# Operand sums, gate quarters and sample attention moved to other places in a written-out order

## The chip, the cores and the metric

The kernel runs on one core of a Trainium2 chip. The metric is the device time of one execution in microseconds. TensorE (PE, with PEld for its weight loads) multiplies, VectorE (DVE) and ScalarE (ACT) do the elementwise work, and SyncE (SP) issues every DMA. "L97" in the profile is the line of a helper that records nearly all operations, so the rows are told apart by the names of their tiles.

## The reference

One layer of a hybrid decoder for 1024 prompt positions and 8 samples of 8 new tokens, 1088 rows in all. With `x` of width 2048:

```python
proj = jnp.einsum('bld,de->ble', x, w_in)
gb, gc, h, z_c, q, k, v, z_a, gate_c, gate_a = jnp.split(proj, SPLIT_OFFSETS, axis=-1)
conv_out, conv_state = short_conv(gc * h, conv_prev, conv_w)
y_c = jax.nn.silu(z_c) * gb * conv_out
o, k_state, v_state = attend_fn(q, k, v)
y_a = jax.nn.silu(z_a) * o
merged = (jax.nn.sigmoid(gate_c) * jnp.einsum('blc,cd->bld', y_c, w_conv_out)
          + jax.nn.sigmoid(gate_a) * jnp.einsum('bla,ad->bld', y_a, w_attn_out))
out = jnp.einsum('bld,de->ble', merged, w_out)
y = layer_norm(ALPHA * x + out, ln_g, ln_b)
```

Attention has 16 heads of 64 on 4 key heads, a window of 128, sinks and ALiBi. Samples also read cached keys and values, and the updated caches are outputs.

## The kernel before

**Units.** The projections are made by 100 units that run one after the other. Each is a 2 x 2 block product done with seven products in place of eight (sums of blocks on both sides). In units a0 to a41 half of the input channels are multiplied, for 42 pairs of column blocks; in b0 to b41 the other half is added; m0_0 to m0_7 and m1_0 to m1_7 multiply the convolution's and the attention's result by their output weights. A product is 24 matmuls of 128 x 272 in four *groups* of six, so a unit has 28 groups. Every number is split into a high and a low part, and a product takes three matmuls for a block. The tiles follow the names: `psa37a`, `psa37b` and `psa37c` are the three accumulators of unit a37, `wra`, `wrb` and `wrm` raw weights, `wa`, `wb` and `wm` split weights, `wsa` and so on their sums, `ca`, `cb` and `cm` the unit's result, `xab`, `xdb`, `xcb` and `xbb` the four operand blocks of stage b and `xam` to `xbm` those of stage m.

**Order.** The class `InOrder` wraps PE, DVE, ACT and SP's queue (`te`, `ve`, `se`, `dq`): each engine issues in the order in which the program is written. `tick()` stands behind each group, counts it in `clock`, runs what the agenda has for this number (`after(n, f)`: n groups from now), and takes one piece from `line`, a list of small DVE and ACT steps. So an instruction that waits for a DMA on DVE holds up all that is written behind it for DVE. In `run`, weights are split three products ahead of their use; a product's accumulator is taken out (`take`) after the first group of the next product, and products 2, 4 and 6 add to the accumulator that has just been taken out, so they wait for it. A unit's raw weights are loaded in the third group of the unit before.

**Operands.** `ahead_of(ops)` loads the four blocks of an operand, 16 loads of 272 KB, and puts the eight sums of `combine` on `line`. It is called by the `begin` of a37 (for stage b), of b23 (`gate_unit(13, open_merge)`, for m0) and of m0_4 (for m1). The operand is split into its seven forms (`put`) during the last unit before its stage: a41, b25 and m0_7.

**Merge.** In m0 and m1 each quarter of a unit's result that is finished (by products 1, 4, 5 and 6) is multiplied on DVE by a quarter of the sigmoid gates (`sg`), and in m1 the quarter of m0's result (`cmo`) is added. `gated` issues these loads from its `taken`, which is called when a product is taken out. The last products' results go to `mgd`, from which the output projection (tiles `yr`, `m`, `ms`, weights `wraw` and `wo`, sums `o`) reads.

**Attention and samples.** Prompt attention runs between the units' groups, in 64 steps 15 groups apart. Step s loads its query and key tiles (`qt`, `kt`) at its start, multiplies scores (`sc`) 14 groups later, loads values (`vt`) at 22 and uses them (`po`) at 34. Beside the first eight gate units, b10 to b17, eight sample steps run; each is begun by `after(16, ...)` from its unit's `begin`. The first opens the pool of samples too: it transposes the new keys and values and issues `store`, ten groups after, which writes the caches with 20 DMAs, two of them whole-cache copies in DRAM (`out_k_s<-in_ck`, `out_v_s<-in_cv`).

Of the kernel before, what the change touches and what calls it, by code (L numbers as in the profile page):

```python
# [9 lines left out]
F32 = mybir.dt.float32  # L10
# [7 lines left out]
P = 128  # L18
# [6 lines left out]
HALF = T // 2  # L25
# [25 lines left out]
def tile_hybrid_step(  # L51
# [8 lines left out]
    def pool(name, bufs=1, space=None, stack=None, side=None):  # L60
        kw = {} if space is None else {"space": space}
        if side is not None:
            kw["side"] = side
        if space is not DRAM:
            kw["reuse_waits"] = "tile"
        return (stack or ctx).enter_context(tc.tile_pool(name=name, bufs=bufs, **kw))
# [54 lines left out]
    def at(step, what):  # L121
        assert step > clock[0]
        agenda.setdefault(step, []).append(what)

    def after(groups, what):
        at(clock[0] + groups, what)
# [33 lines left out]
    def slot(shape, dt, name):  # L160
        i = turn_of[0] % (NX if ring[1] is None else SLOTS)
        turn_of[0] += 1
        full = ring[i >= NX].tile([P, T], dt, name=name, tag=f"slot{i}")
        return full[:, : shape[0] * shape[1]].rearrange("p (a b) -> p a b", a=shape[0])

    class Operands:
# [29 lines left out]
        def combine(self, k):  # L196

            line.append(lambda: ve.tensor_sub(self.t3[k], self.t2[k], self.t3[k]))
            line.append(lambda: ve.tensor_add(self.t2[k], self.t3[k], self.b11[k]))
# [227 lines left out]
    def ahead_of(ops):  # L427

        ops.load_all()
        for k in range(4):  # L430
            ops.combine(k)

    todo = []
    for p in range(2, len(PAIRS)):
# [10 lines left out]
    pools = {}  # L445
# [124 lines left out]
    class Step:  # L570
# [116 lines left out]
        def gated(self):  # L687
            ve.tensor_mul(self.o, self.o, self.sz)
            dq.dma_start(yd[8 + self.j][:, TS + self.blk * P : TS + (self.blk + 1) * P], self.o)
# [9 lines left out]
    def gate(d, c):  # L699
        def sigmoid(f):  # L700
            se.activation(c[:, f], c[:, f], AF.Sigmoid)

        after(1, lambda: sigmoid(0))
        after(4, lambda: sigmoid(1))
        after(6, lambda: dq.dma_start(sgd[d], c))
# [4 lines left out]
    def open_samples():  # L710
        sp = pools["sample"] = pool("sample", stack=sam)
        kn = late["kn"] = sp.tile([TS, 2, P], F32, name="kn")
        vn = late["vn"] = sp.tile([TS, 2, P], F32, name="vn")

        tn = late["tn"] = sp.tile([32, 160], F32, name="tn")
        ve.memset(tn, 0.0)
        kl = sp.tile([P, 2, P], F32, name="kl")
        klast, vlast, qkvs, ident = (late[n] for n in ("klast", "vlast", "qkvs", "ident"))

        def turned(i):  # L720
            t = aux(f"pko{i}")
            te.transpose(t[:, 0:P], klast[:, i, :], ident)
            te.transpose(t[0:TS, P : 2 * P], qkvs[:, 8 + i, :], ident)
            te.transpose(t[0:TS, 2 * P : 3 * P], qkvs[:, 10 + i, :], ident)

            def copies():
                se.copy(kl[:, i, :], t[:, 0:P])
                se.copy(kn[:, i, :], t[0:TS, P : 2 * P])
                se.copy(vn[:, i, :], t[0:TS, 2 * P : 3 * P])

            after(2, copies)

        def store():
            dq.dma_start(k_p, kl.rearrange("p a b -> p (a b)"))
            dq.dma_start(v_p, vlast.rearrange("p a b -> p (a b)"))
            for src, old, dst in ((kn, ck, k_s), (vn, cv, v_s)):
                for b in range(NS):
                    dq.dma_start(
                        dst[b, WIN - ST :, :],
                        src[b * ST : (b + 1) * ST].rearrange("p a b -> p (a b)"),  # L740
                    )
                dq.dma_start(dst[:, : WIN - ST, :], old[:, ST:, :])

        after(2, lambda: turned(0))
        after(6, lambda: turned(1))
        after(10, store)
# [200 lines left out]
    def project(p, end, begin=None):  # L947
        u = Unit(f"b{p}", win[p, 1], x1, add=pd[p], begin=begin, end=end)
        todo.append(u)
        return u  # L950
# [19 lines left out]
    def gate_unit(d, begin=None):  # L970
        return project(GT + d, lambda c: gate(d, c), begin)

    def samples(i):
        if i == 0:
            heads_st.close()
            open_samples()
        sample(i // 2, i % 2)

    for i in range(8):
        gate_unit(i, lambda i=i: after(16, lambda: samples(i)))  # L980
    gate_unit(8)

    def open_conv():
# [15 lines left out]
            gate_unit(9 + ct // 2)  # L999


    mst = ExitStack()
    xm = [None, None]

    def open_merge():
        con.close()
        keep.close()
        pools["merge"] = pool("merge", side="right")
        stage = pool("mstage", stack=mst, side="right")
        for b in range(2):  # L1010
            xm[b].stage = stage
        ahead_of(xm[0])
# [4 lines left out]
    gate_unit(14)  # L1017
    x1.leaves = (gate_unit(15), xm[0])

    def gated(b, i):  # L1020

        pos = {1: (0, 0), 4: (1, 1), 5: (1, 0), 6: (0, 1)}
        tiles = {}

        def fetch(q):
            f, h = pos[q]
            hs = slice(h * HALF, (h + 1) * HALF)
            t = tiles[q] = [pools["merge"].tile([P, HALF], F32, name=f"sg{b}_{i}_{q}", tag="sg", bufs=2)]
            dq.dma_start(t[0], sgd[i + 8 * f][:, b, hs])
            if b:  # L1030
                t.append(pools["merge"].tile([P, HALF], F32, name=f"cmo{i}_{q}", tag="cmo", bufs=2))
                dq.dma_start(t[1], cmd[i][:, f, hs])

        def taken(u, n):
            if n == 0:
                fetch(1)
            if n == 2:
                fetch(4)
            if n == 3:
                fetch(5)  # L1040
            if n == 4:
                fetch(6)
            if n not in pos:
                return
            f, h = pos[n]
            v = u.c[:, f, h * HALF : (h + 1) * HALF]
            t = tiles.pop(n)
            after(1, lambda: ve.tensor_mul(v, v, t[0]))
            if b:
                after(2, lambda: ve.tensor_add(v, v, t[1]))  # L1050
            if n == 6:
                after(3, lambda: dq.dma_start((mgd if b else cmd)[i], u.c))

        return taken

    def open_out():
        mst.close()
        pools["oraw"] = pool("oraw", side="right")

    for b, w in enumerate((wc, wa)):  # L1060
        for i in range(8):
            u = Unit(f"m{b}_{i}", w[i], xm[b], taken=gated(b, i))
            if (b, i) == (0, 4):
                u.begin = lambda: ahead_of(xm[1])
            if (b, i) == (0, 7):
                xm[0].leaves = (u, xm[1])
            if (b, i) == (1, 1):
                u.begin = open_out
            todo.append(u)
# [5 lines left out]
    ps, mq = PS["ps"], pools["oraw"]  # L1075

    def split(hi, lo, raw):
        nc.scalar.copy(hi, raw)  # L1078
        nc.vector.tensor_sub(lo, raw, hi.bitcast(F32))  # L1079
# [4 lines left out]
    ORDER = [k for i in range(8) for k in (i, i + 8)]  # L1084

    def weight(k, n):
        raw = mq.tile([P, 512], F32, name="wraw", tag="wraw", bufs=3)
        nc.sync.dma_start(raw, wo[k * P : (k + 1) * P, n * 512 : (n + 1) * 512])
        w = wpool.tile([P, 2, 512], F32R, name="wo", tag="w", bufs=5)
        split(w[:, 0], w[:, 1], raw)  # L1090
        return w[:, 0], w[:, 1]

    units.close()
    op = pool("out")
    ring[1] = op
# [4 lines left out]
    def operand(gi, k):  # L1100
        t0, tn = GROUPS[gi]
        raw = mq.tile([P, tn], F32, name=f"yr{gi}_{k}", tag="yr", bufs=3)
        nc.sync.dma_start(raw, mgd[k % 8][:, k // 8, t0 : t0 + tn])
        m = slot([2, 512], F32R, f"m{gi}_{k}")
        skip = tn - 512
        split(m[:, 0], m[:, 1], raw[:, skip:])
        if skip:
            split(ms[:, k, 0:TS], ms[:, k, TS:], raw[:, 0:TS])
        return m
# [96 lines left out]
    m = {k: operand(0, k) for k in ORDER}  # L1206
# [20 lines left out]
    for i, o in enumerate(outs):  # L1227
        t = clock[0] + 1 + 3 * i
# [16 lines left out]
        for o, a in zip(outs, acc):  # L1245
            o.residual(n, a)
    for k in ORDER:
        raw = mq.tile([P, 512], F32, name="wraw", tag="wraw", bufs=3)
        nc.sync.dma_start(raw, wo[k * P : (k + 1) * P, 3 * 512 :])
        if len(last) < 12:  # L1250
            w = slot([2, 512], F32R, f"l{k}")
        else:
            w = wpool.tile([P, 2, 512], F32R, name=f"l{k}", tag="w", bufs=5)
        split(w[:, 0], w[:, 1], raw)
        last[k] = w
    for i, o in enumerate(outs):
        halves = (slice(0, 256), slice(256, 512)) if i == 3 else (slice(0, 512),)
        for h, c in enumerate(halves):
            acc = banks(f"o1_3_{i}_{h}", 1)[0]
            for kk, k in enumerate(ORDER):  # L1260
                w = last[k]
# [81 lines left out]
```

## Time and profile before

| | |
|---|---|
| three runs | 2747.66 us median, 2744.4 to 2748.97 |
| profiled execution | 2749.23 us, span 2747.1 us |
| mean granted clock of TensorE | 0.988 |
| PE busy | 2646.6 us, 96% |
| DVE busy | 1756.7 us, 64% |
| ACT busy | 1058.9 us, 39% |
| DMA | 415.97 MB, mean 151 GB/s |

In a list of waits, a row says which engine with which tile waited for whom, then the total in us, the times, and the longest. In a timeline, a row has the start, the length, the engine, line and operation, the tiles, and in brackets the idle time of the engine before it and what ended it. In a table of stretches, the columns are the busy time and number of instructions of PE, PEld, DVE, ACT and POOL, and then the granted clock, the busy share of the DMA engines and GB/s.

### The profile page before, as it was taken

Reading aid. Unit: us, or ns where it says so; the run is one execution under the profiler, and the core shown is the slowest. Engines: PE = TensorE matmul, PEld = TensorE weight load, DVE = VectorE, ACT = ScalarE, POOL = GpSimd, SP = SyncE. Lnnn points to the kernel's source line nnn. Section 1 sums busy time; section 2 is a strip of 40 time slices with the busy share of each in tenths; the row PEclk is TensorE's granted clock in tenths of the full one; section 3 lists DMA queues with packets and bytes.
Section 4 is the critical chain, followed back from the end, with each engine's and each line's share of the span. In section 5 each row is a group of like instructions: output and inputs, shape, how many; then the busy total and the mean of one; then the engine's idle time right before and its main releaser. Section 6 shows DMA issues by size and latency. Waiting matters only on the chain.

```text
span 2747.1 us, 47820 instructions
## 1 busy us (share of the span) xinstructions
PE 2646.6 (96%) x19426; PEld 2548.5 (93%) x19426; DVE 1756.7 (64%) x3371; ACT 1058.9 (39%) x2074; POOL 0.2 (0%) x4
## 2 busy tenths in 40 slices
PE   8999999999989999989999999998999999899997
PEld 7999999999989999989989999998999999688886
DVE  7444444444444878878878898887765877533836
ACT  5222322232223446555654555543432423322221
POOL 0000000000000000000000000000000000000000
PEclk9999999999999999999999999999999999999999
DMA  4322332232242366665554545445345566733543
GB/s 161 110 96 96 114 109 96 96 118 105 96 160 96 142 214 207 203 196 164 185 165 141 176 145 163 160 154 202 139 144 209 195 212 199 254 98 113 182 141 103
DMA packets 167328, 415.97 MB, mean 151 GB/s; under 512 B 23443, under 2 KB 75667, under 8 KB 139173
## 3 DMA queue, kind: packets, MB, share of 16 engines
q1 hardware_dynamic: 167108, 412.92, 45.1%
q8 instruction: 153, 2.51, 0.4%
q14 instruction: 67, 0.54, 0.1%
HBM read 295.33 MB, written 119.48 MB: 151 GB/s over the span
## 4 chain that ended last, share of the span: by engine, by line
PE 73%; DVE 14%; ACT 6%; DMA 5%; issue 2%; SPq 1%; DVEq 0%; ACTq 0%
PE o L97 11%; DVE cb L97 2%; DVE wb L97 1%; DMA yr<-mgd 1%; ACT wb L97 1%; ACT p L97 1%; DMA wraw<-in_wo 1%; PE psm_5a L97 1%; PE psm_1a L97 1%; PE psm_6a L97 1%; PE psm_2a L97 1%; ACT L97 1%; PE psm_4a L97 1%; DVE nm L97 1%; DVE wsb L97 1%
## 5 line engine op out<-in xcount | busy, mean ns | idle before, releaser
L97 PE MATMUL o<-wo,m 128*128 128x512 f32 x1344 | 320.9, 394 | 0.2 <-DVE r L1156 0.2
L97 PEld LDWEIGHTS o<-wo,m 128*128 128x128 f32 x1344 | 255.0, 190 | 56.0 <-issue 0.6
L97 DVE TENSOR_TENSOR wa<-wra,wa 128x512 fp32r<-128x512 f32 x210 | 144.4, 689 | 213.3 <-ACT wa L97 213.3
L97 ACT CAST wb<-wrb 128x512 fp32r<-128x512 f32 x210 | 127.3, 615 | 158.3 <-DVE wrb L97 153.4
L1079 DVE TENSOR_TENSOR wo<-wraw,wo 128x512 fp32r<-128x512 f32 x112 | 76.7, 687 | 150.8 <-ACT wo L1078 150.8
L97 DVE TENSOR_TENSOR wb<-wrb,wb 128x512 fp32r<-128x512 f32 x210 | 143.6, 684 | 42.8 <-ACT wb L97 41.1
L1078 ACT CAST wo<-wraw 128x512 fp32r<-128x512 f32 x112 | 69.3, 621 | 222.3 <-PE o L97 173.5
L97 ACT CAST wa<-wsa 128x512 fp32r<-128x512 f32 x84 | 52.2, 621 | 259.4 <-DVE wsa L97 259.4
L97 ACT CAST wa<-wra 128x512 fp32r<-128x512 f32 x210 | 126.3, 621 | 49.2 <-DVE wra L97 47.2
L97 DVE TENSOR_TENSOR wa<-wsa,wa 128x512 fp32r<-128x512 f32 x84 | 58.0, 691 | 92.3 <-ACT wa L97 92.2
L97 ACT CAST wb<-wsb 128x512 fp32r<-128x512 f32 x84 | 51.6, 614 | 155.9 <-DVE wsb L97 154.0
L97 ACT ACTIVATE p<-p,nm 128x256 f32<-128x256 f32 (+1 forms) x128 | 62.4, 489 | 83.7 <-DVE nm L97 83.6
L97 DVE TENSOR_TENSOR wb<-wsb,wb 128x512 fp32r<-128x512 f32 x84 | 57.7, 687 | 33.2 <-ACT wb L97 33.0
L97 ACT ACTIVATE p<-p,den 128x256 f32<-128x256 f32 (+1 forms) x128 | 56.5, 489 | 58.1 <-DVE den L97 56.6
L97 ACT ACT_TABLE_LOAD x58 | 74.4, 1283 | 1.7 <-PEq L1321 0.7
L97 ACT CAST wm<-wrm 128x512 fp32r<-128x512 f32 x80 | 48.4, 621 | 60.9 <-DVE wrm L97 60.7
L97 DVE TENSOR_TENSOR wm<-wrm,wm 128x512 fp32r<-128x512 f32 x80 | 55.1, 688 | 25.2 <-ACT wm L97 24.4
L97 DVE TENSOR_TENSOR cm<-cm,sg 128x544 f32<-128x544 f32 x64 | 46.3, 724 | 33.3 <-DMA sg<-sgd 32.1
L97 ACT CAST wm<-wsm 128x512 fp32r<-128x512 f32 x32 | 19.9, 621 | 104.2 <-DVE wsm L97 98.4
L97 PEld LDWEIGHTS first<-xa,wa 128*128 128x128 f32 x336 | 46.2, 203 | 13.1 <-ACT wa L97 6.0
L97 PE MATMUL first<-xa,wa 128*128 128x272 f32 x336 | 47.8, 305 | 10.2 <-ACT wa L97 4.3
L97 DVE TENSOR_TENSOR o<-po,ot 64x128 f32<-64x128 f32 x128 | 36.0, 281 | 24.5 <-ACT ot L97 23.4
(1072 smaller groups left out, 6512.0 us busy)
## 6 DMA issues: line engine op xcount, KB each, us to landing
pd<-ca SPq DMA_DIRECT2D x42, 1088.0 KB
cb<-pd SPq DMA_DIRECT2D x42, 1088.0 KB
wra<-in_win SPq DMA_DIRECT2D x42, 1024.0 KB
wrb<-in_win SPq DMA_DIRECT2D x42, 1024.0 KB
wraw<-in_wo SPq DMA_DIRECT2D x128, 256.0 KB
sgd<-cb SPq DMA_DIRECT2D x16, 1088.0 KB
sg<-sgd SPq DMA_DIRECT2D x64, 272.0 KB
qt<-qd SPq DMA_DIRECT2D x128, 128.0 KB
```

Source lines behind the costliest of these rows:

```text
L97: first = f(*args, **kw)
L1078: nc.scalar.copy(hi, raw)
L1079: nc.vector.tensor_sub(lo, raw, hi.bitcast(F32))
```

## The change

- `ahead_of` still issues the 16 loads at once, but puts the sums on `line` 34 groups later.
- `gated` fetches quarter 1 of a unit's gates after product 5 of the unit before (for m0_0 at its `begin`), in place of after its own product 0; quarter 4 after product 1 in place of 2, quarter 5 after 2 in place of 3, quarter 6 after 3 in place of 4. The quarters have three buffers in place of two.
- The sample steps begin 20 groups after their units in place of 16.
- The pool of the quarters lies on the left side of the on-chip memory in place of the right, and is closed before the output projection; the output weights' raw tiles (`wraw`) have four buffers in place of three.

```diff
@@ ahead_of @@
         ops.load_all()
-        for k in range(4):
-            ops.combine(k)
+
+        def combine():
+            for k in range(4):
+                ops.combine(k)
+
+        after(34, combine)
@@
-        gate_unit(i, lambda i=i: after(16, lambda: samples(i)))
+        gate_unit(i, lambda i=i: after(20, lambda: samples(i)))
@@ open_merge @@
-        pools["merge"] = pool("merge", side="right")
+        pools["merge"] = pool("merge", stack=mgs)
@@ gated @@
-            t = tiles[q] = [pools["merge"].tile([P, HALF], F32, name=f"sg{b}_{i}_{q}", tag="sg", bufs=2)]
+            t = tiles[q] = [pools["merge"].tile([P, HALF], F32, name=f"sg{b}_{i}_{q}", tag="sg", bufs=3)]
             dq.dma_start(t[0], sgd[i + 8 * f][:, b, hs])
             if b:
-                t.append(pools["merge"].tile([P, HALF], F32, name=f"cmo{i}_{q}", tag="cmo", bufs=2))
+                t.append(pools["merge"].tile([P, HALF], F32, name=f"cmo{i}_{q}", tag="cmo", bufs=3))
                 dq.dma_start(t[1], cmd[i][:, f, hs])
 
+        def early():
+            fetch(1)
+
         def taken(u, n):
-            if n == 0:
-                fetch(1)
-            if n == 2:
-                fetch(4)
-            if n == 3:
-                fetch(5)
-            if n == 4:
-                fetch(6)
+            if n in (1, 2, 3):
+                fetch((4, 5, 6)[n - 1])
+            if n == 5 and nxt:
+                nxt()
@@
+    takers, nxt = {}, None
+    for b in (1, 0):
+        for i in reversed(range(8)):
+            takers[b, i], nxt = gated(b, i, nxt)
     for b, w in enumerate((wc, wa)):
         for i in range(8):
-            u = Unit(f"m{b}_{i}", w[i], xm[b], taken=gated(b, i))
+            u = Unit(f"m{b}_{i}", w[i], xm[b], taken=takers[b, i])
+            if (b, i) == (0, 0):
+                u.begin = nxt
@@ weight, and the last block's weights @@
-        raw = mq.tile([P, 512], F32, name="wraw", tag="wraw", bufs=3)
+        raw = mq.tile([P, 512], F32, name="wraw", tag="wraw", bufs=4)
...
+    mgs.close()
     units.close()
     op = pool("out")
```

More of the change, by code (lines that the diff above doesn't have):

```diff
@@ L999, in tile_hybrid_step @@
             gate_unit(9 + ct // 2)
-    mst = ExitStack()
+    mst, mgs = ExitStack(), ExitStack()
     xm = [None, None]
@@ L1018, in tile_hybrid_step, with gated @@
     x1.leaves = (gate_unit(15), xm[0])
-    def gated(b, i):
+    def gated(b, i, nxt):
         pos = {1: (0, 0), 4: (1, 1), 5: (1, 0), 6: (0, 1)}
@@ L1052, in taken @@
                 after(3, lambda: dq.dma_start((mgd if b else cmd)[i], u.c))
-        return taken
+        return taken, early
     def open_out():
@@ L1247, in tile_hybrid_step @@
     for k in ORDER:
-        raw = mq.tile([P, 512], F32, name="wraw", tag="wraw", bufs=3)
+        raw = mq.tile([P, 512], F32, name="wraw", tag="wraw", bufs=4)
         nc.sync.dma_start(raw, wo[k * P : (k + 1) * P, 3 * 512 :])
```

## The prediction

> **What bounds the kernel.** The page first: what limits the span.
>
> ```profile
> span 2747.1 us, 47820 instructions
> ...
> PE 2646.6 (96%) x19426; PEld 2548.5 (93%) x19426; DVE 1756.7 (64%) x3371; ACT 1058.9 (39%) x2074; POOL 0.2 (0%) x4
> ```
>
> TensorE (PE) is busy 96% of 2747.1 us. The change removes no matmul, so it can only win from the 100 us in which PE stands, and from matmuls that run slowly after standing. Next the waits of PE (total, times, longest):
>
> ```profile
> PE psa37a L97 <- ACT ca L97: 11.7, 1, 11.7
> ...
> PE psb23a L97 <- DVE cb L97: 7.1, 1, 7.1
> PE o L97 <- DVE ms L1079: 6.5, 2, 4.9
> ...
> PE psm_4a L97 <- ACT cm L97: 5.6, 1, 5.6
> PE sc L97 <- DVE tn L97: 4.5, 1, 4.5
> ...
> PE o L97 <- DVE l L1079: 1.4, 4, 0.7
> ```
>
> The first, second and fourth fall in units a37, b23 and m0_4: exactly the units whose `begin` calls `ahead_of`. The waits of all engines say why:
>
> ```profile
> ACT wa L97 <- DVE wra L97: 47.2, 44, 15.9
> ...
> DVE cm L97 <- DMA sg<-sgd: 32.1, 14, 3.7
> ...
> DVE xbb L97 <- DMA xbb<-in_xt: 14.6, 1, 14.6
> DVE xbm L97 <- DMA xbm<-yd: 14.5, 2, 7.3
> ```
>
> VectorE (DVE) stands 14.6 us once and 7.3 twice at most on an operand that has only just been asked for. It works in order, so weights and accumulators behind that sum wait, ScalarE (ACT) waits for DVE, PE for both. DVE's 32.1 us on gate quarters (`sg`) is larger, but in the stage m0/m1 no wait of PE goes with it, except at its end (below).
>
> **The three operand sums.** PE's first matmuls of units give the price, since a unit with no trouble, b24, takes 1951.97 - 1930.88 = 21.09 us (28 groups of 0.75 us, seven products of 3.01 us).
>
> ```profile
> 801.91 3.17 PE L97 MATMUL psa37a<-xa,wa 128*128 128x272 f32 x24
> ...
> 837.70 2.55 PE L97 MATMUL psa38a<-xa,wa 128*128 128x272 f32 x19
> 1900.44 3.17 PE L97 MATMUL psb23a<-xb,wb 128*128 128x272 f32 x24
> ...
> 1930.88 3.18 PE L97 MATMUL psb24a<-xb,wb 128*128 128x272 f32 x24
> ...
> 1951.97 3.17 PE L97 MATMUL psb25a<-xb,wb 128*128 128x272 f32 x24
> ...
> 1973.64 3.18 PE L97 MATMUL psm_0a<-xm,wm 128*128 128x272 f32 x24
> ...
> 2063.96 3.18 PE L97 MATMUL psm_4a<-xm,wm 128*128 128x272 f32 x24
> ...
> L97 PE MATMUL psm_5a<-xm,wm x192: 286/288/291, 2092.2 to 2290.4; 128*128 128x272 f32 x192
> ```
>
> a37 took 35.79, 14.70 too much; b23 30.44, 9.35 too much; m0_4 28.24, 7.15 too much: 31.2 us in all, slow matmuls included. The sums move 34 groups, at least 25.5 us; the loads were there after 14.6 us, so these waits go entirely. The loads are issued as before.
>
> What is late next? In a37 the next weights are issued behind the 16 operand loads, and they were in nobody's way only because everything stood.
>
> ```profile
> 814.29 0.33 SPq L97 DMA_DIRECT2D wra<-in_win  x1
> ...
> 821.00:822.00 1.00, 1.00 (x7) 1.00 (x6) 0.97 (x3) 0.00 (x0) 0.00 (x0) 0.50 0.02 8
> ...
> 828.86 0.61 ACT L97 COPY ca<-psa37b 128x544 f32<-128x544 f32 x1 [2.04 <-PE psa37b L97]
> 829.37 1.14 ACT L97 CAST wa<-wra 128x512 fp32r<-128x512 f32 x2
> 830.02 0.69 DVE L97 TENSOR_TENSOR wa<-wra,wa 128x512 fp32r<-128x512 f32 x1 [2.48 <-ACT wa L97]
> ...
> 831.87 0.72 DVE L97 TENSOR_TENSOR ca<-ca,psa37a 128x544 f32<-128x544 f32 x1 [1.16 <-PE psa37a L97]
> ...
> 1982.69 4.79 PE L97 MATMUL psm_0a<-xm,wm 128*128 128x272 f32 x24 [2.85 <-ACT cm L97]
> ```
>
> The DMA row (last columns: clock, DMA share, GB/s) is quiet from 821 on: a38's weights, last in the queue, have just landed. With 0.7 for the word of it, which no row shows, I take 821.7. The queue does not depend on PE, so this stays. Without the stall product 4 begins at 801.91 + 4 x 3.01 = 813.96; ACT takes psa37b and then wants a38's first weight (rows 828.86, 829.37). It waits till 821.7, casts (0.61); DVE, which stands at the low half (0.69), then takes psa37a out (0.72): 823.9. Product 6 accumulates on that bank and could start at 819.99. So 3.9 us of stall remain. Standing lowers the clock: after 2.85 us idle, 24 matmuls took 4.79 instead of 3.18, 1.6 more; I add 1.5. Left over 5.4, gain in a37 14.70 - 5.4 = 9.3. [...]
>
> In b23 and m0_4 the next weights are queued behind operand loads too:
>
> ```profile
> 1906.13 0.34 SPq L97 DMA_DIRECT2D wrb<-in_win  x1
> ...
> 2070.36 0.33 SPq L97 DMA_DIRECT2D wrm<-in_wc  x1
> ```
>
> They are issued 5.7 and 6.4 us into their units, a38's 12.4 us into a37: some 6 us sooner, more than the 3.9 us by which a38's are late. So no new stall there: 9.35 and 7.15 whole, at the other end 4 less each, as in a37.
>
> The eight sums of 0.72 us now go one per group among running work. The row nearest is unit b25, where operand pieces also come one per group for most of a unit: 1973.64 - 1951.97 = 21.67, 0.58 more than free. A third of that, 0.2 each, 0.6 in all (ends 0 and 0.58 each).
>
> **Gate quarters.** No DVE work is added; 96 loads are issued earlier and three buffers mean that `fetch(6)` no longer waits for the product with quarter 4. The next unit's quarter 1 takes the buffer of quarter 4, multiplied three groups before, so SP's queue isn't held longer than now. On it the quarters pass the weights' loads and the stores of `cm`; before m0_4 one more stands ahead of the 16 operand loads of the same size, a sixteenth of some 14 us, which the 34 groups cover. Within the stage I cost it at nothing: DVE is not what PE waits for there. At the last unit it is:
>
> ```profile
> 2332.90 0.61 ACT L97 COPY cm<-psm_7a 128x544 f32<-128x544 f32 x1 [2.35 <-PE psm_7a L97]
> ...
> 2335.51 0.72 DVE L97 TENSOR_TENSOR cm<-cm,sg 128x544 f32<-128x544 f32 x1 [2.69 <-DMA sg<-sgd]
> ```
>
> The last multiplication can begin when ACT's copy ends (2333.5) instead of 2335.51: 1.9 us, straight on PE's path, since DVE makes `ms` behind it and PE waits for `ms` (6.5 us above). The fourth `wraw` buffer and the pool moved and closed earlier: between 0 and the 1.4 us for `l`; 0.5.
>
> **Samples four groups later.** These rows are of b11. The store of the sample caches begins when ACT has copied `kl`; it ends with a whole-cache copy, and everything behind it on SP's queue is late.
>
> ```profile
> 1179.02 0.27 ACT L97 COPY kl<-pko 128x128 f32<-128x128 f32 x1 [0.15 <-PE pko L97]
> ...
> 1183.98 0.58 ACT L97 CAST pp<-pt 128x512 fp32r<-128x512 f32 x1
> ...
> 1192.15 0.70 SPq L97 DMA_DIRECT2D out_v_s<-in_cv  x1
> ...
> 1194.80 0.42 SPq L97 DMA_DIRECT2D wrb<-in_win  x1
> ...
> 1195.79 0.37 SPq L97 DMA_DIRECT2D vt<-vcd  x1
> ...
> 1202.00:1208.00 6.00, 4.96 (x22) 5.00 (x23) 4.44 (x13) 1.82 (x3) 0.00 (x0) 0.50 0.84 327
> ...
> 1203.04 1.19 PE L97 MATMUL sc<-kt,qt 128*128 128x256 f32 x4 [4.52 <-DVE tn L97]
> ...
> 1206.16 0.62 ACT L97 CAST wb<-wrb 128x512 fp32r<-128x512 f32 x1 [2.52 <-DMA wrb<-in_win]
> ...
> 1209.68 0.64 PE L97 MATMUL po<-pp,vt 128*128 128x256 f32 x4
> ```
>
> Groups are counted from the kernel's start: b10, the first gate unit, is the 53rd unit of 28 and begins at group 1456. Today `qt` (attention step 14, due at 1484) is behind the store (due 1482), and its scores wait 4.52 us; 6 us at half clock lose 3.0 more: 7.5. After the change the store is due at 1486, so `qt` passes it and this wait goes. But `vt` of step 13 (due 1491, used at 1503) stays behind. The copies of `kl` then stand behind the cast at 1183.98, so the store begins 5.6 us later, and the whole-cache copy is issued at about 1197.8. Weights `wrb` come 14.0 us after that issue now (1206.16), less some 2.5 for `qt` and `kt` that are no longer between (my estimate, from the 3.1 us between the scores at 1203.04, which need both, and the weights): 1209.3. The gate's store (1088 KB) and `vt` are queued behind them; if `vt` lands with the weights' first parts, at 1206.5, it stalls PE 4.3 us (`po` would be due at 1209.68 - 7.5 = 1202.2) plus 3.0 of slow clock, a loss of nothing against 7.5; if last, near 1212, 9.8 + 3.0, a loss of 5.3. If it isn't late at all, 7.5 are won. I take a loss of 4, since it is issued behind both; ends +7.5 and -6. The other seven samples shift against attention steps of 15 groups without any row that says which way: 0, ends 3 us either way.
>
> **Sum.** 9.3 + 9.35 + 7.15 - 0.6 + 1.9 + 0.5 - 4 = 23.6 us. The profiled execution took 2749.23 us (span 2747.1), which gives 2725.6; it lies 1.57 above the median of the runs shown, 2747.66, which gives 2724.1. I say 2724.
>
> **Rivals.**
> 1. *Nothing takes the removed waits' place*: a38's weights land in time and `vt` isn't late. For it: no row gives a single load's landing, and both rest on a landing. Against it: one queue serves all, and both stand behind megabytes. Then 14.70 + 9.35 + 7.15 - 0.6 + 1.9 + 0.5 + 7.5 = 40.5: 2707; one of the two alone, 2712 to 2719.
> 2. *The queue takes more back*: weights of b24 and m0_5 stall as a38's do (4 each), `vt` costs 6, the sums 0.58 each, the shifted samples 3. 23.6 - 8 - 2 - 1.1 - 3 = 9.5: 2738.
> 3. *Slower*: early gate fetches hold SP's in-order queue in front of the merge units' weights. From 1.7 us in each of 14 units on, 23.6 us are gone; if each got the wait of the row at 1982.69, 2.85 and 1.6 for the clock, it would be 62 us: 2786. Against: each fetch finds a buffer whose product was multiplied two products before, and today's `fetch(6)`, which does wait, costs no unit anything.
> 4. *It does not do what it says*: the sums still meet loads that are not there, or DVE stands at the next operand: 2745 to 2750. The 14.6 us against 25.5 speak against it.
>
> **How the numbers follow.** Forecast 0.50 (own range 2718 to 2731), rival 1 0.22 (with its half cases), rival 2 0.18, rival 3 0.05, rival 4 0.05. The range 2711 to 2738 leaves out the full rival 1, rivals 3 and 4: 0.2. A measurement here tells about 0.2%, 5.5 us, from no change. Faster: forecast, 1 and 2, most of 4 not: 0.91; within 0.2% 0.05; slower 0.04.
>
> **What would show it.** No wait of DVE on `xbb` or `xbm`; a37 at some 26 us with ACT waiting on `wra`; b23 and m0_4 within 1 us of 21.09; PE's wait at `o` down to about 3; in b11 no wait before `sc` but one before `po`, with `vt` behind the cache copy. Wrong I would be first where a DMA lands: a38's weights before 817, or `vt` before 1202.

## The result, and the profile after

The changed kernel takes 2725.78 us (median of 4 runs, 2724.45 to 2726.72) against 2747.57 us (4 runs, 2744.4 to 2748.97): a ratio of 0.9922, 95% interval 0.9905 to 0.9939, so 21.8 us faster. The profiled execution took 2725.17 us with a span of 2723.1, 24.0 us less than the span before. The forecast was 2724, with 23.6 us for the span.

The page of the changed kernel, and then its waits of PE (total, times, longest):

```profile
span 2723.1 us, 47823 instructions
...
PE 2639.6 (97%) x19426; PEld 2545.0 (93%) x19426; DVE 1757.8 (65%) x3371; ACT 1057.7 (39%) x2074; POOL 0.2 (0%) x4
```

```profile
PE po L97 <- DMA vt<-vcd: 9.0, 1, 9.0
...
PE psa37a L97 <- DVE ca L97: 4.8, 1, 4.8
PE o L97 <- DVE ms L1088: 4.2, 2, 2.9
```

Of the three waits in a37, b23 and m0_4 one is left, 4.8 us instead of 11.7. The one before `sc` is gone, and one before `po`, 9.0 us, is new. DVE no longer waits at `xbb` or `xbm`, and at `sg` only once, 1.3 us, where it was 32.1 us in all. What has grown is ACT's waiting at weights, from 2.0 and 2.5 us in all before to:

```profile
ACT wa L97 <- DMA wra<-in_win: 10.0, 2, 8.1
ACT wb L97 <- DMA wrb<-in_win: 9.2, 2, 7.2
```

Where the time came from is read from the first matmuls of units, as in the prediction. Each of these rows groups a unit's matmuls on one accumulator in the changed kernel (shortest, median, longest in ns, then first and last start in us; the rows of m hold m0 and m1):

```profile
L97 PE MATMUL psa37a<-xa,wa x96: 287/288/596, 801.9 to 830.1; 128*128 128x272 f32 x96
L97 PE MATMUL psa38a<-xa,wa x96: 286/288/291, 830.2 to 851.2; 128*128 128x272 f32 x96
L97 PE MATMUL psb11a<-xb,wb x96: 282/287/429, 1179.4 to 1217.6; 128*128 128x272 f32 x96
L97 PE MATMUL psb12a<-xb,wb x96: 285/288/391, 1217.7 to 1243.7; 128*128 128x272 f32 x96
L97 PE MATMUL psb23a<-xb,wb x96: 286/288/291, 1901.5 to 1922.5; 128*128 128x272 f32 x96
L97 PE MATMUL psb24a<-xb,wb x96: 286/288/291, 1922.6 to 1943.6; 128*128 128x272 f32 x96
L97 PE MATMUL psm_4a<-xm,wm x192: 286/288/292, 2055.7 to 2253.7; 128*128 128x272 f32 x192
L97 PE MATMUL psm_5a<-xm,wm x192: 286/288/292, 2076.8 to 2274.8; 128*128 128x272 f32 x192
```

Each stretch runs from the first start of one row to that of another, read in the same way in both traces:

| stretch | before, us | after, us | won | predicted |
|---|---|---|---|---|
| a37 | 35.8 | 28.3 | 7.5 | 9.3 |
| b0, b1 | 49.0 | 50.7 | -1.7 | 0 |
| b10 up to b23 (samples) | 741.9 | 748.8 | -6.9 | -4 |
| b23 | 30.4 | 21.1 | 9.3 | 9.35 |
| m0_4 | 28.2 | 21.1 | 7.1 | 7.15 |
| m0_5 up to the first `o` | 245.6 | 243.4 | 2.2 | 1.9 |
| first `o` to the end | 409.3 | 402.9 | 6.4 | 0.5 |
| units with the moved sums (a38, b24, m0_5) | 3 x 21.1 | 3 x 21.1 | 0 | -0.6 |

These add up to 23.9 of the 24.0 us. The sum was met, but three of its terms were too small or too large by 1.8, 2.9 and 5.9 us, and one stretch was not foreseen. The experiments were made for those terms.

The two new waits, in order of time (start, duration, engine, operation, in brackets the idle time and what ended it). First a37 in the changed kernel:

```profile
815.15 0.33 SPq L97 DMA_DIRECT2D wra<-in_win  x1
...
822.92 1.14 ACT L97 CAST wa<-wra 128x512 fp32r<-128x512 f32 x2 [8.12 <-DMA wra<-in_win]
823.57 0.69 DVE L97 TENSOR_TENSOR wa<-wra,wa 128x512 fp32r<-128x512 f32 x1 [10.54 <-ACT wa L97]
824.18 0.71 DVE L97 TENSOR_TENSOR ca<-ca,psa37a 128x544 f32<-128x544 f32 x1
...
824.95 5.40 PE L97 MATMUL psa37a<-xa,wa 128*128 128x272 f32 x24 [4.77 <-DVE ca L97]
```

The chain is the predicted one: a38's weights land late, ACT stands 8.12 us at the cast, DVE behind it, and the accumulator is taken out late. The landing is at 822.9, not 821.7, so PE stands 4.77 us and not 3.9; and the 24 matmuls behind it take 5.40 us instead of the 3.18 of a free row, 2.2 and not 1.5.

Then b11 in the changed kernel:

```profile
1181.40 0.81 SPq L97 DMA_DIRECT2D out_k_s<-in_ck  x1
1182.31 7.63 SPq L97 DMA_DIRECT2D out_v_s<-vn  x8
...
1189.98 0.72 SPq L97 DMA_DIRECT2D out_v_s<-in_cv  x1
1190.76 0.43 SPq L97 DMA_DIRECT2D wrb<-in_win  x1
1191.31 0.35 SPq L97 DMA_DIRECT2D sgd<-cb  x1
1191.76 0.37 SPq L97 DMA_DIRECT2D vt<-vcd  x1
...
1192.88 0.64 PE L97 MATMUL sc<-kt,qt 128*128 128x256 f32 x4
...
1203.14 0.62 ACT L97 CAST wb<-wrb 128x512 fp32r<-128x512 f32 x1 [7.25 <-DMA wrb<-in_win]
...
1206.23 1.19 PE L97 MATMUL po<-pp,vt 128*128 128x256 f32 x4 [8.96 <-DMA vt<-vcd]
1207.22 1.56 PE L97 MATMUL psb11a<-xb,wb 128*128 128x272 f32 x6
```

`sc` no longer waits. `vt` stands behind the second cache copy, the weights and the gate's store, and its product waits 8.96 us. The second copy was issued at 1189.98, not at the predicted 1197.8; b10 itself started 5.8 us earlier than before, so against the units' starts the difference is 2.0 us. `po` started at 1206.23, which with these 5.8 is the late one of the two landings that the prediction weighed (near 1212). From its first start to b12's, b11 takes 38.3 us, where it took 33.2 before.

### The profile page after: what moved, and what is told of

It reads as the page before. It is cut to its first block, busy times and chain, and to the rows that moved or that the text cites. A ratio compares the mean times of both kernels' runs of the same rounds, so it can differ in the third digit from the quotient of the medians.

```text
span 2723.1 us, 47823 instructions
## 1 busy us (share of the span) xinstructions
PE 2639.6 (97%) x19426; PEld 2545.0 (93%) x19426; DVE 1757.8 (65%) x3371; ACT 1057.7 (39%) x2074; POOL 0.2 (0%) x4
## 5 line engine op out<-in xcount | busy, mean ns | idle before, releaser
L97 DVE TENSOR_TENSOR o<-po,ot 64x128 f32<-64x128 f32 x128 | 35.9, 280 | 27.1 <-ACT ot L97 26.0
L97 DVE TENSOR_TENSOR pp<-pt,pp 128x512 fp32r<-128x512 f32 (+1 forms) x64 | 41.7, 651 | 12.9 <-ACT pp L97 12.8
```

Of the source, the lines that this page charges most:

```text
L97: first = f(*args, **kw)
```

## The experiments

Each kernel is the changed kernel with the edit shown, but for the sums alone, which start from the kernel before. Times are medians of 4 runs (10 for the kernel with the gate quarters alone) beside the kernel before on the same chip: 2748.22 for the first four, 2747.29 for the next three, 2747.37 for the last two. Medians of two edited kernels may be from different chips; these three medians of the kernel before are within 1 us of each other. The table shows the stretches of every kernel's trace, by the same first starts as above.

| kernel | median, us | ratio, 95% interval | a37 | b0, b1 | b10 to b23 | b23 | m0_4 | m0_5 to `o` | `o` to end |
|---|---|---|---|---|---|---|---|---|---|
| before | 2747.57 | 1 | 35.8 | 49.0 | 741.9 | 30.4 | 28.2 | 245.6 | 409.3 |
| after | 2725.78 | 0.9922 (0.9905 to 0.9939) | 28.3 | 50.7 | 748.8 | 21.1 | 21.1 | 243.4 | 402.9 |
| samples at 16 | 2718.42 | 0.9890 (0.9875 to 0.9905) | 28.5 | 50.6 | 741.9 | 21.1 | 21.1 | 243.4 | 404.6 |
| sums alone | 2733.59 | 0.9945 (0.9928 to 0.9962) | 28.4 | 50.6 | 740.9 | 21.1 | 28.4 | 245.2 | 408.4 |
| three `wraw` | 2729.01 | 0.9930 (0.9914 to 0.9946) | 28.5 | 49.1 | 745.4 | 21.1 | 21.1 | 243.8 | 408.8 |
| gates alone | 2745.6 | 0.9991 (0.9981 to 1.0001) | 35.9 | 49.0 | 738.5 | 30.3 | 28.2 | 243.4 | 409.1 |
| weights first | 2717.23 | 0.9891 (0.9876 to 0.9906) | 21.0 | 48.9 | 745.1 | 21.0 | 21.1 | 243.5 | 405.1 |
| copies early | 2715.6 | 0.9888 (0.9868 to 0.9908) | 28.3 | 50.5 | 739.9 | 21.1 | 21.0 | 243.4 | 403.5 |
| copies early, samples at 16 | 2717.59 | 0.9892 (0.9877 to 0.9907) | 28.0 | 49.4 | 739.8 | 21.1 | 21.1 | 243.4 | 406.4 |
| both mends | 2709.13 | 0.9866 (0.9849 to 0.9882) | 21.1 | 49.1 | 739.5 | 21.1 | 21.1 | 243.5 | 403.1 |
| sums and gates | 2724.52 | 0.9919 (0.9904 to 0.9933) | 28.6 | 50.3 | 741.9 | 21.1 | 21.1 | 243.4 | 407.7 |

**Samples back at 16 groups.**

```diff
-        gate_unit(i, lambda i=i: after(20, lambda: samples(i)))
+        gate_unit(i, lambda i=i: after(16, lambda: samples(i)))
```

> The changed kernel with the samples back at 16 groups. Theory (the move to 20 only turned the wait before the scores of step 14 into a longer one before the output of step 13, and cost about 6.9 us between b10 and b26): 2725.8 - 6 = about 2719.5, with a wait of PE of some 4 to 5 us before sc in b11 and none over 1 us before po. Rival (the loss in this stretch comes from units reaching it 5.8 us earlier, not from the 20): within 2 us of 2725.8. Second rival (the move is worth something after all): slower than 2728.

2718.42 us: moving the samples costs 7 us. The wait before `sc` is back in the trace (4.9 us) and the one before `po` gone; b11 takes 33.2 us again, against 38.3.

**The sums alone.** The kernel before with the new `ahead_of` and nothing else:

```diff
         ops.load_all()
-        for k in range(4):
-            ops.combine(k)
+
+        def combine():
+            for k in range(4):
+                ops.combine(k)
+
+        after(34, combine)
```

> The kernel before with only the operand sums 34 groups later. Theory: 7.5 (a37 keeps a wait for a38's weights) + 9.4 + 7.1 less some 1 to 2 lost in b0 to b9 gives 2747.6 - 22.5 = about 2725, the whole of the measured change by itself. Rival (sums at the new place or fetches in the old order take part of it back in m0 and m1): 2730 or more. Rival (weights of a38 not late without the other edits): 2717.

2733.59 us: the rival's number. a37 and b23 win what they win in the changed kernel, but m0_4 still takes 28.4 us. Its trace shows what took the place of the wait for `xbm`:

```profile
2050.92 3.06 SPq L97 DMA_DIRECT2D xbm<-yd  x4
...
2055.78 16.45 SPq L97 DMA_DIRECT2D sg<-sgd  x4
...
2066.10 0.73 DVE L97 TENSOR_TENSOR cm<-cm,sg 128x544 f32<-128x544 f32 x1 [10.67 <-DMA sg<-sgd]
2068.64 0.61 ACT L97 COPY cm<-psm_4b 128x544 f32<-128x544 f32 x1
...
2069.30 4.75 PE L97 MATMUL psm_4b<-xm,wm 128*128 128x272 f32 x24 [5.59 <-ACT cm L97]
```

The unit's first gate quarter is issued in the unit itself, behind the 16 operand loads, and DVE stands 10.67 us at it. In the kernel before, DVE stood 7.13 us at `xbm`, then made the sums, and came to the quarter just before it landed, so that only 0.19 us of this wait showed:

```profile
2073.18 0.72 DVE L97 TENSOR_TENSOR xbm<-xcm,xbm 128x544 f32<-128x544 f32 x1 [7.13 <-DMA xbm<-yd]
...
2081.11 0.73 DVE L97 TENSOR_TENSOR cm<-cm,sg 128x544 f32<-128x544 f32 x1 [0.19 <-DMA sg<-sgd]
```

**Three `wraw` buffers.** Both places with `bufs=4` set back:

```diff
-        raw = mq.tile([P, 512], F32, name="wraw", tag="wraw", bufs=4)
+        raw = mq.tile([P, 512], F32, name="wraw", tag="wraw", bufs=3)
```

> The changed kernel with three buffers for the raw output weights again. Theory (the fourth buffer is what shortens the output projection by 3.0 us before its last block and 3.4 us in it): 2725.8 + 6 = about 2732, with PE waits for l of about 2 us back. Rival (the gain there comes from starting with the last gate quarter in place, or from chance clock dips): 2725.8, at most 2 us more.

2729.01 us, 3.2 slower than the changed kernel: between the expectation (6) and its rival (at most 2). The place shows clearly in the matmuls with the last weights `l`. First the kernel with three buffers, with what PE waited for there; then the changed kernel, where only the waits for `r`, which both have, are left; then the kernel before:

```profile
L97 PE MATMUL o<-l,m x240: 277/389/743, 2663.4 to 2714.0; 128*128 128x512 f32 x72, 128*128 128x256 f32 x48
...
  DVE l L1088: 0.7, 3
  ACT l L1087: 0.7, 1
```

```profile
L97 PE MATMUL o<-l,m x240: 276/389/500, 2664.9 to 2711.4; 128*128 128x512 f32 x72, 128*128 128x256 f32 x48
...
  DVE r L1166: 1.6, 2
```

```profile
L97 PE MATMUL o<-l,m x240: 276/389/502, 2685.5 to 2735.4; 128*128 128x512 f32 x72, 128*128 128x256 f32 x48
```

From first to last start these are 50.6, 46.5 and 49.9 us. In the kernel before, the 3.4 us over the changed kernel are 2.0 us of waits for `l` (1.4 for DVE, 0.6 for ACT) and 1.4 us of PE's busy time: the waits cut the matmuls into five runs of one to three, and such a run takes about 0.26 us longer than as many matmuls in a long row (0.96 us for three, where 96 take 22.43). The granted clock stays at 1.00 over these 49.9 us.

With three buffers and the other edits, the 4.1 us are 1.3 us more of standing and 2.8 us more of busy time, because here the clock dips as well. The kernel of the experiment after next (sums and gate quarters together, also with three buffers) has the same waits without a dip. The ten us around the waits (length, then busy time of PE, PEld, DVE, ACT and POOL, granted clock, DMA share, GB/s), and the 96 matmuls behind them, first in the kernel with three buffers:

```profile
2674.00:2684.00 10.00, 8.12 (x26) 5.70 (x26) 7.47 (x19) 0.91 (x2) 0.00 (x0) 0.83 0.01 3
...
2677.86 23.98 PE L97 MATMUL o<-l,m 128*128 128x512 f32 x96 [0.78 <-DVE r L1166]
```

then in that with sums and gate quarters:

```profile
L97 PE MATMUL o<-l,m x240: 279/389/505, 2660.7 to 2709.8; 128*128 128x512 f32 x72, 128*128 128x256 f32 x48
...
2671.30:2681.30 10.00, 8.11 (x32) 5.78 (x32) 7.47 (x19) 0.91 (x2) 0.00 (x0) 1.00 0.01 5
...
2675.18 22.41 PE L97 MATMUL o<-l,m 128*128 128x512 f32 x96 [0.78 <-DVE r L1166]
```

PE stands for 1.9 of the 10 us in both, and the clock is 0.83 in one and 1.00 in the other; the dip costs 1.6 us. It is in three of the five kernels with three buffers. From the first matmul with `l` to the end of the span these five take 60.7 to 63.3 us, the six with four buffers 58.1 to 58.5.

**The gate quarters alone.** The changed kernel with `ahead_of` making its sums at once, the samples at 16 and three `wraw`.

> The kernel before with only the gate quarters fetched earlier, with three buffers, their pool on the other side and closed earlier (sums, samples and output weights as before). Theory: only the start of the output projection moves, by 1.9 us: 2745.7. Rival (the 32 us that VectorE waits for these quarters do cost PE something in m0 and m1): 2740 or less. Rival (earlier fetches hold the queue in front of weights): 2750 or more.

2745.6 us, within what can be told from no change. The trace has the 2.2 us between m0_5 and the first `o`, and m0_4 at its old 28.2: the earlier quarters alone do nothing for that unit.

**Sums and gate quarters together.** The changed kernel with the samples at 16 and three `wraw`.

> The kernel before with the operand sums 34 groups later and the gate quarters fetched earlier with three buffers, but the samples at 16 groups and three buffers of raw output weights, both as before. Theory that unit m0_4 is freed only by the two together: sums alone 2733.6 less 2 us at the output projection less the 7 us of m0_4: 2723 to 2725, and if the fourth buffer is worth the 3.2 us measured with the samples at 20, the kernel with samples at 16 (2718.4) plus 3.2: 2721.6. In the trace m0_4 takes 21.1 us with no wait of PE at psm_4b. Rival that the parts simply add: sums alone 14.6 and gates alone 2.6 off 2748.2, 2731, with m0_4 at 28.

2724.52 us, and m0_4 at 21.1. Each against the kernel before on the same chip, sums alone won 14.6 us and gates alone 2.6, together 17.2; the kernel with both wins 22.9, 5.6 more. In its trace m0_4 is 7.1 us shorter than before, which neither edit does alone.

**a38's weights ahead of the operand loads.**

```diff
+    def weights_first():
+        todo[38 - 2].load()
+        ahead_of(x1)
...
-            begin={2: one_by_one, 37: lambda: ahead_of(x1)}.get(p),
+            begin={2: one_by_one, 37: weights_first}.get(p),
```

> The changed kernel with the raw weights of a38 asked for before the 16 operand loads of stage b instead of behind them. Theory (what is left of the stall in a37, 28.3 us against 21.1, is those weights being last in the queue): a37 takes 21.1 us and the time is 2725.8 - 7 = about 2718.7. Rival (the operand loads or the store of a36 then become the next late thing, or the sums 34 groups later meet loads that aren't there): 2723 or more, with a wait of VectorE on xbb.

2717.23 us. Its trace in a37:

```profile
802.97 0.42 SPq L97 DMA_DIRECT2D wra<-in_win  x1
...
814.52 1.14 ACT L97 CAST wa<-wra 128x512 fp32r<-128x512 f32 x2
814.63 2.86 SPq L97 DMA_DIRECT2D xbb<-in_xt  x4
...
817.02 0.72 DVE L97 TENSOR_TENSOR ca<-ca,psa37a 128x544 f32<-128x544 f32 x1 [1.16 <-PE psa37a L97]
```

The weights are issued at 802.97 instead of 815.15, the cast waits for no DMA, and the unit takes 21.0 us. So the whole rest of a37 was the late landing and its slow clock. The sums find `xbb` in time although it is loaded last.

**The whole-cache copies early.** The copies don't depend on the samples, so they are issued at two quiet places of stage a; the 18 small stores stay.

```diff
-                dq.dma_start(dst[:, : WIN - ST, :], old[:, ST:, :])
...
+    def old_rows(old, dst):
+        dq.dma_start(dst[:, : WIN - ST, :], old[:, ST:, :])
+
+    at(300, lambda: old_rows(ck, k_s))
+    at(350, lambda: old_rows(cv, v_s))
```

> The changed kernel with the two whole-cache copies in DRAM issued in stage a, 300 and 350 groups from the start, and the 18 small stores left where they are. Theory (vt comes late because it stands behind these two copies on SP's queue): b11 takes about 26 us in place of 38.3, no wait of PE before po, 2725.8 - 12 = about 2714. Rival (the 18 small stores hold the queue by themselves): 2722 or more, with the wait before po still over 4 us.

2715.6 us. b11 takes 28.7 us, and the same part of the trace now reads:

```profile
1182.03 2.64 SPq L97 DMA_DIRECT2D out_v_s<-vn  x8
...
1185.03 0.36 SPq L97 DMA_DIRECT2D wrb<-in_win  x1
...
1189.10 0.37 SPq L97 DMA_DIRECT2D vt<-vcd  x1
...
1197.68 0.64 PE L97 MATMUL po<-pp,vt 128*128 128x256 f32 x4
```

No wait before `po`. The eight stores of `vn` leave the queue in 2.64 us where they took 7.63 behind the first copy.

**The copies early and the samples at 16.** Both edits.

> As the run before, and the samples back at 16 groups. Theory (the wait before the scores at 16 has the same cause as the one before po at 20): 2718.4 - 7.5 = about 2711, no wait over 1.5 us before sc in b11; what is left between this run and the run before, some 3 us, is the place of the other seven samples. Rival (at 16 the scores wait for something else): 2717 or more.

2717.59 us, no better than with the samples at 20; about 2711 was expected. The wait before `sc` in b11 is gone, as expected, and b11 takes 29.6 us. The 3 us that the expectation added for the other seven samples came from a comparison of single traces. From b10 to b23 both kernels take the same, 739.8 and 739.9 us. But single traces don't settle whether 16 or 20 is better here: from b18's first matmul to b19's this one takes 129.4 us, against 126.5 in the kernel with the samples at 16 and the copies in place. PE's waits are the same in both (1.9 us the longest), while over 14 us around them the granted clock is 0.82 in one and 1.00 in the other.

**Both mends.** a38's weights first and the copies early, with the samples at 20.

> The changed kernel with both mends together: in a37 the weights of a38 are loaded ahead of the 16 operand loads, and the two whole-cache copies are issued at groups 300 and 350 of stage a, with only the 18 small stores of the samples left behind them. Theory: the two mends touch stretches of the kernel 350 us apart and share no wait, so their gains add: 2725.8 - 8.6 (weights alone, 2717.2) - 10.2 (copies alone, 2715.6) = 2707, between 2704 and 2711. In the trace a37 takes 21.0 us and b11 below 30. Rival: the copies, issued in stage a, delay weights there, or stage b falls into its other alignment, and half of one gain is lost: 2711 to 2717.

2709.13 us, ratio 0.9866 (0.9849 to 0.9882): it is faster than both kernels, and within the intervals the gains add: 8.6 and 10.2 us alone, 16.7 together. a37 takes 21.1 us, b10 to b23 739.5. The first rival (nothing takes the removed waits' place) had put the time at 2707; with these two further edits it comes within 2.1 us of that.

## Why the prediction was right

**The path and the waits.** Right: three units stood because DVE, in order, stood at an operand just asked for, and 34 groups were enough in each.

**a37, 9.3 predicted, 7.5 measured.** The mechanism held, and is shown: with the weights early the wait is gone. The size was off by 1.8. The landing was 1.2 us later than taken, 0.9 of it because the weights were issued that much later than before. The 0.7 for the word of it, for which the prediction had no row, fits: in the changed kernel the last traffic is at 822.1 to 822.2 and the cast starts at 822.92. The slow clock cost 2.2 and not 1.5. (The steps that the prediction adds to 821.7 give 823.7, not 823.9, a slip of 0.2 us the other way.)

**b23, 9.35.** Right: PE has no wait there. ACT does wait 1.9 us for b24's weights, too short a time to reach PE.

**m0_4, 7.15.** The number was right by luck, since a step was wrong. The prediction gave it to the sums alone and costed the gate quarters "within the stage" at nothing, since "DVE is not what PE waits for there". With the sums moved DVE is what PE waits for in that unit, at the gate quarter behind the 16 operand loads; the sums alone leave 28.4 us, the quarters alone 28.2, both 21.1. The change held the second edit for another reason. The question "what is late next" was asked of the weights and not of DVE's own next operand.

**The moved sums.** Predicted 0.2 us each, and nothing shows: in the changed kernel a38, b24 and m0_5 take 21.1 us each, as before.

**The gate quarters at the end, 1.9.** Right (the two times that it subtracts are 2.0 apart, and 2.2 were won). From m0_5 to the first `o` the nine kernels that fetch them early take 243.4 to 243.8 us, the two that don't 245.2 and 245.6. The row of the first `o`:

```profile
2320.18 0.69 PE L97 MATMUL o<-wo,ms 128*128 128x512 f32 x2 [2.92 <-DVE ms L1088]
```

It still waits 2.92 us, where it was predicted to wait about 3.

**The fourth `wraw`, 0.5 predicted with 1.4 as the upper end.** Too small, and outside its bounds. By the medians it is worth 3.2 us. From the first matmul with `l` to the end the five kernels with three buffers take 62.0 us on average, the six with four 58.2: 3.8 us. The bound counted PE's waits for DVE's `l` alone. It left out 0.6 us of waits for ACT, the 1.4 us by which the matmuls take longer when waits cut them into short runs, and the dip of the clock in some kernels.

**The samples, -4 predicted between +7.5 and -6.** Right in mechanism, `vt` behind the copies, and shown by the copies alone: moved away, the wait goes. The size: -6.9 in the profiled pair, just outside the ends. 5.1 of it is b11, and the prediction had 5.3 for `vt` landing last; it chose a loss between its two landings (the early one, 1206.5, is not worked out from a row), and the late one came. Between the five kernels with the samples at 16 and the copies in place (mean 741.0 us from b10 to b23) and the three with 20 (mean 746.4) it is -5.4, of which 5.0 in b11. Outside b11 the five take 707.3 to 708.8 us and the three 708.0 to 710.5, so the other seven samples, put at 0, move too little to tell.

**Not foreseen: b0 and b1, -1.7.** These two units take 48.9 to 49.4 us in six of the eleven kernels and 50.3 to 50.7 in five, with no edit there that would divide them. In the changed kernel PE waits a little for DVE's `cb` several times. The four kernels in which a37 has no wait for late weights are all among the six; of the seven that have it, two are. What sets it is open. Similarly the stretch from the first `o` to the first `l` took 344.7 to 347.9 us without an edit that explains it.

**The sum.** That 23.9 us met 23.6 is in part luck. Against their terms, a37, b0 and b1, and the samples lost 6.4 us, and the stretch from the first `o` to the end won 5.9 more than its 0.5. Of the 6.4 us won there, 3.4 lie behind the first `l`, where the fourth buffer acts. The other 3.0 lie between the first `o` and the first `l`, in the stretch that differs by as much without an edit that explains it; without them the pair would differ by about 21 us.

## What to carry to other kernels

When a wait of an in-order engine is taken away, list what that engine reads next and where its load stands in the queue: the second wait can lie under the first, and the views hardly show it until the first is gone (0.19 us before, 10.67 after). A price for a wait of TensorE takes in the slower matmuls beside it: 2.2 us on top of 4.8 in a37, where the clock fell, and 1.4 on top of 2.0 at `l` in the kernel before, where it did not. Two single traces can differ by 3 us at the same waits, so a term of that size needs several kernels. A large transfer with no dependence on the work around it belongs where the queue is quiet, and the load needed next goes ahead of a block of loads needed later; these two edits, of a few lines, gave 16.7 us beyond the change.

## What the runs showed of the hardware

**The clock after a pause.** Rows of the changed kernel by stretch (columns as above): in a37, and behind the wait for `vt`.

```profile
821.00:830.00 9.00, 5.05 (x23) 5.05 (x24) 5.14 (x8) 1.75 (x3) 0.00 (x0) 0.62 0.02 6
...
1206.00:1212.00 6.00, 5.77 (x26) 5.80 (x27) 3.01 (x10) 1.80 (x4) 0.00 (x0) 0.50 0.94 265
```

Around 4.77 us of standing the granted clock is 0.62 over nine us, and after 8.96 it is 0.50 for the next six. A third of the loss in a37 is this and not the wait. By single us the clock there is 0.94 from 822, 0.50 from 823 to 829, and 1.00 again from 830: it fell some 2.7 us after PE's last matmul (820.2). Before the late `vt` it fell some 4.5 us after the last matmul (1197.27; 0.75 from 1201.5, 0.50 from 1202). At the 2.85 us pause of the kernel before, ahead of the row at 1982.69, it fell some 3.2 us after (1979.84; 0.53 from 1983, 0.50 from 1984 to 1986), when PE was working again. What sets these delays no run shows.

**The clock at short waits.** The clock also fell without one long pause. With three `wraw` buffers PE's waits around the first matmuls with `l` are 0.78 us at most, and the granted clock of the ten us is 0.83; at the same waits in another kernel it is 1.00 (the rows above). What decides between them no run shows.

**Copies within the chip's memory on the same queue.** The 960 KB copies of the caches held up what was issued behind them by several us: eight 8 KB stores took 7.63 us to leave the queue behind one, 2.64 without it. The weights behind the second copy were at ACT 12.4 us after their issue (1190.76 to 1203.14). Issued in stage a (the first at 234.8 us, in the changed kernel at 1181.40) the same two copies cost nothing that shows: a37 starts at 802.6 in the kernel with the copies early, and between 801.6 and 803.0 in the eleven traces.
